# First channel group of the pooling mixer: pooled without scale and shift, both applied later, and TensorE, ScalarE and VectorE in written order there

## The chip, the core and the metric

The kernel runs on one core of a Trainium2 chip. The metric is the device time of one execution in microseconds (us), the median of several. Engines: TensorE (PE) multiplies matrices, VectorE (DVE), ScalarE (ACT) and GpSimd (POOL) work elementwise, SyncE (SP) issues the DMA transfers from HBM.

## What is computed

Two layers of a backbone over 256 latent tokens and 256 context tokens with 2048 channels, float32. Layer 0 mixes tokens by pooling in four channel groups of 512 (windows 2, 4, 8, 16), layer 1 by attention; a gated MLP with a depthwise convolution follows each. What matters here is the start of layer 0:

```python
ml = (silu_c @ w_mod[i] + b_mod[i]).reshape(B, 6, 1, D)      # shift, scale, gate; shift, scale, gate
mc = (silu_cc @ w_mod[i] + b_mod[i]).reshape(6, 1, 1, D)
a_lat = modulate(rms_norm(h, norm1_g[i]), ml[:, 0], ml[:, 1])   # x * (1 + scale) + shift
...
parts.append(window_sum / count[None, :, None] - ug)          # pool_mix, per channel group
y = jnp.einsum('btgc,gcd->btgd', p, w).reshape(B, T, D) + b
return y * scale
...
h = h + ml[:, 2] * y_lat
h = h + ml[:, 5] * conv_ffn(modulate(rms_norm(h, norm2_g[i]), ml[:, 3], ml[:, 4]), ...)
```

The pooling is linear along the tokens, and scale and shift are one number per channel: pool(s * x + t) = s * pool(x) + t * pool(1).

## The kernel before

Channels lie on the 128 partitions: a stream (latent `hl`, context `hc`) is 16 tiles of 128 x 256, and both streams are worked on together as 128 x 512. Float32 products are made of three matmuls with high and low parts (hi x hi, hi x lo, lo x hi); `split` (L143, L145) makes the parts of weights with a cast on ScalarE and a difference on VectorE.

The modulation is a product with w_mod, 24 chunks of 512 channels. `mod_pe` makes one chunk: eight loads ("pieces") of 512 KB, `wm{layer}_{chunk}_{g}_{0 or 1024}`; each piece gives two matmuls with 32 columns of output each (L193), and the piece `..._0` fills other columns of the array (j = 0, 1) than `..._1024` (j = 2, 3). The bank is then evicted by ScalarE (L198, `modev`), transposed by TensorE (L203, `modt`), reduced and biased on VectorE (L205, L181, and L183 for scales) to `modT`. Chunk 4w + g belongs to group g; w = 0 is the shift, 1 the scale, 2 the gate, 4 the second scale; 12 + g is the second shift. `mods()` lists the chunks, `need(n)` advances this list to its n-th step of four per chunk.

`mixer(g)` pools one group: `py` = h x scale x rs1 on VectorE (L453; rs1 is one over the norm), the shift added by ScalarE into a zero-padded row `pad` (L455), window sums `ws` on VectorE (L461), times one over the count on GpSimd (`pf`, L466), minus the middle (L467), high and low parts `ph` (L469, L470). Then 48 matmuls with the pooling weights `wp` (`pm`, L484 to L486), eviction with gate and bias by ScalarE (`pz`, L491), the addition to h by GpSimd (L493), squares for the second norm (`n2q`, L276), and `Ad`, h times the second scale in two parts (L502, L503). `partial(g)` multiplies `Ad` with the first columns of the MLP's weights (`cg`, `cu`, L545 to L547), and in between calls `need` and the next step of the next group's mixer; `pw` (L528) and `pt` (L561) are its products with the second shift.

Loads go through SP's queue in order, into "rooms" (`stage`): 6 of a pool of their own and those of the tiles A0 to A15 that `lend` names. A load waits until the last user of its room is done. The order of all engines is set by a planner that works on the list of operations with estimated times; nothing in this part is written out by hand.

Of the kernel before, what the change touches and what calls it, by code (L numbers as in the profile page):

```python
# [10 lines left out]
F32 = mybir.dt.float32  # L11
F32R = mybir.dt.float32r
# [45 lines left out]
def kernel(ctx: ExitStack, tc: tile.TileContext, xT, cxT, wmod, wg, wu, wd, wp,  # L58
# [264 lines left out]
    with ExitStack() as ph0:  # L323
# [62 lines left out]
        with ExitStack() as phs:  # L386
# [4 lines left out]
            n1 = Norm(both, f0, "n1")  # L391
            for k in range(KT):
                n1.add(h_of, k)
            pr = n1.rstd()
            rs1 = st.tile([P, 512], F32, bufs=1, name="rs1")
            nc.scalar.copy(rs1, pr)
# [42 lines left out]

            def mixer(g):  # L440
# [4 lines left out]
                gsc = st.tile([P, 8], F32, bufs=1, name=f"gsc{g}")  # L445
                gbi = st.tile([P, 8], F32, bufs=1, name=f"gbi{g}")
                pa = []
                for i in range(4):
# [7 lines left out]
                    src, w = pad, 1  # L456
                    while w < win:
                        n = WP - 2 * w + 1
                        if w == 1:
                            dst = st.tile([P, 2, WP], F32, tag="ws", name=f"ws{k}")  # L460
                        nc.vector.tensor_tensor(dst[:, :, :n], src[:, :, :n], src[:, :, w : w + n], op=ALU.add)  # L461
                        src, w = dst, 2 * w
                    o = PAD - win // 2
                    pf = f0.tile([P, 2, T], F32, tag="t2", name=f"pf{k}")
                    for s in both:
                        nc.gpsimd.tensor_tensor(pf[:, s, :], src[:, s, o : o + T], inv_t, op=ALU.mult)  # L466
                    nc.vector.tensor_tensor(pf, pf, pad[:, :, PAD : PAD + T], op=ALU.subtract)  # L467
                    ph = ap0.tile([P, 2, 2, T], F32R, tag=f"A{k}", name=f"ph{k}")
                    nc.scalar.copy(ph[:, 0], pf)  # L469
                    nc.vector.tensor_tensor(ph[:, 1], pf, ph[:, 0].bitcast(F32), op=ALU.subtract)  # L470
                    pa.append(ph)
                    if i == 3:
                        parts = ld(wp[g], f"wp{g}")
                    yield
                nc.vector.tensor_tensor(gsc, modT[0, 8 + g].rearrange("p i s -> p (i s)"), V("ps")[:, 8 * g : 8 * g + 8],
                                        op=ALU.mult)
                nc.vector.tensor_tensor(gbi, gsc, V("pb")[:, 8 * g : 8 * g + 8], op=ALU.mult)
                for m in range(4):
                    ps = bank("d", f"pm{g}_{m}")
                    for i in range(4):  # L480
                        hi, lo = parts[i // 2]
                        c = 512 * (i % 2) + P * m
                        rh, rl = flat(pa[i][:, 0]), flat(pa[i][:, 1])
                        nc.tensor.matmul(ps, hi[:, c : c + P], rh, start=(i == 0), stop=False)  # L484
                        nc.tensor.matmul(ps, hi[:, c : c + P], rl, start=False, stop=False)
                        nc.tensor.matmul(ps, lo[:, c : c + P], rh, start=False, stop=(i == 3))  # L486
                    k = 4 * g + m
                    y = f0.tile([P, 2, T], F32, tag="t2", name=f"pz{k}")
                    for s in both:
                        j = 2 * m + s  # L490
                        nc.scalar.activation(y[:, s], ps[:, T * s : T * s + T], AF.Identity,  # L491
                                             scale=gsc[:, j : j + 1], bias=gbi[:, j : j + 1])
                        nc.gpsimd.tensor_tensor(h_of(s)[:, k, :], h_of(s)[:, k, :], y[:, s], op=ALU.add)  # L493
                    n2.add(h_of, k)
                    if m % 2:
                        yield

# [714 lines left out]
```

## Time and profile before

| | |
|---|---|
| median of 3 runs | 3119.4 us (3118.2 to 3119.62) |
| the profiled execution | 3121.16 us, its span 3119.4 us |
| mean granted TensorE clock | 0.992 |
| TensorE waiting for pieces of w_mod | 25.3 us in 14 waits, the longest 19.0 us (the start) |
| HBM read | 554.93 MB, 179 GB/s over the span |

The profile is of one execution. Times are counted from the start of its span. A row of the timeline or of the chain has a start, a duration, an engine, a line and tiles (output<-inputs, with buffer numbers left out); x8 is eight instructions of the profiler, and a float32 matmul shows as two, so a whole piece of w_mod is x4. A name after "<-" at the end is what the engine waited for.

### The profile page before, as it was taken

What the parts mean: (1) busy time and instruction counts of PE and PEld (TensorE: products, weight loads), DVE (VectorE), ACT (ScalarE), POOL (GpSimd) and SP (SyncE); (2) the same over time, 40 slices, a digit from 0 to 9 for tenths busy, and PEclk for the clock granted to TensorE, in tenths of its full rate; (3) what the DMA queues carried; (4) which work ended last, traced back from release to release, by engine and by line L of the source; (5) the groups of instructions that cost most, each with busy time, mean ns of one, the idle gap of its engine ahead of it and who ended that gap; (6) DMA issues with size and microseconds to landing.
All of it is one profiled execution on the core that took longest, in us unless ns stands there. A gap on an engine that the chain in (4) does not pass through costs nothing.

```text
span 3119.4 us, 40851 instructions
## 1 busy us (share of the span) xinstructions
PE 3038.2 (97%) x15082; PEld 2410.6 (77%) x15082; DVE 1937.9 (62%) x2726; ACT 1371.9 (44%) x2219; POOL 874.7 (28%) x845
## 2 busy tenths in 40 slices
PE   6999899999999999999999999999999999999998
PEld 2565558888888888888887888878878888888887
DVE  4445674285765858557485665474767666666666
ACT  3333455323233332333334444343545556566665
POOL 2011213203031130312203000000002576667776
PEclk9999999999999999999999999999999999999999
DMA  9888573374746648476572333333345556555553
GB/s 377 331 273 311 177 237 95 95 231 143 239 150 201 205 148 255 136 215 185 168 249 86 104 113 101 105 110 109 107 149 183 179 173 201 188 183 182 176 191 114
DMA packets 177928, 559.71 MB, mean 179 GB/s; under 512 B 17600, under 2 KB 22208, under 8 KB 177728
## 3 DMA queue, kind: packets, MB, share of 16 engines
q1 hardware_dynamic: 177728, 557.10, 55.1%
q8 instruction: 119, 1.95, 0.2%
q14 instruction: 81, 0.66, 0.1%
HBM read 554.93 MB, written 2.10 MB: 179 GB/s over the span
## 4 chain that ended last, share of the span: by engine, by line
PE 93%; POOL 2%; DVE 2%; DMA 2%; issue 1%; ACT 1%; SPq 0%; DVEq 0%; POOLq 0%; ACTq 0%
PE g L764 5%; PE d L657 5%; PE d L659 5%; PE d L658 5%; PE u L764 5%; PE d L809 4%; PE u L631 4%; PE u L632 4%; PE u L633 4%; PE g L631 4%; PE g L633 4%; PE g L632 4%; PE mod L193 3%; PE g L765 3%; PE u L765 2%; PE d L810 2%
## 5 line engine op out<-in xcount | busy, mean ns | idle before, releaser
L670 POOL TENSOR_TENSOR hl<-hl,dy 128x256 f32<-128x256 f32 x160 | 149.5, 934 | 957.1 <-ACT dy L669 955.9
L241 DVE SCALAR_TENSOR_TENSOR macc<-wm,sc,macc 128x512 f32<-128x512 f32 (+1 forms) x360 | 325.3, 935 | 69.2 <-DMA wm<-wmod 68.0
L821 POOL TENSOR_TENSOR hl<-hl,dy 128x256 f32<-128x256 f32 x320 | 321.3, 1035 | 45.7 <-ACT dy L819 44.1
L669 ACT ACTIVATE dy<-d,modT 128x256 f32<-128x256 f32 x320 | 133.7, 471 | 196.0 <-PE d L659 194.7
L193 PE MATMUL mod<-wm,sc 128*32 128x512 f32 x768 | 135.0, 611 | 25.3 <-DMA wm<-wmod 25.3
L670 POOL TENSOR_TENSOR hc<-hc,dy 128x256 f32<-128x256 f32 x160 | 127.0, 794 | 0.0
L145 DVE TENSOR_TENSOR wd_2l<-wd,wd_2h 128x1024 fp32r<-128x1024 f32 (+1 forms) x44 | 54.8, 1251 | 102.7 <-ACT wd_2h L143 101.8
L819 ACT ACTIVATE dy<-d,modT 128x512 f32<-128x512 f32 x160 | 103.6, 686 | 30.7 <-PE d L810 30.6
L908 POOL TENSOR_TENSOR rk<-rk,rp 128x256 f32<-128x256 f32 x16 | 13.8, 861 | 365.7 <-DVE rk L907 302.0
L466 POOL TENSOR_TENSOR pf<-ws,inv 128x256 f32<-128x256 f32 x32 | 27.8, 887 | 223.8 <-DVE ws L461 156.0
L145 DVE TENSOR_TENSOR wd_3l<-wd,wd_3h 128x1024 fp32r<-128x1024 f32 (+1 forms) x33 | 40.0, 1216 | 80.6 <-ACT wd_3h L143 80.5
L193 PEld LDWEIGHTS mod<-wm,sc 128*32 128x32 f32 x768 | 23.7, 109 | 80.8 <-issue 57.7
L788 DVE TENSOR_TENSOR actb<-sgb,actb 128x256 fp32r<-128x256 f32 x43 | 71.7, 1669 | 21.2 <-ACT actb L787 20.0
L145 DVE TENSOR_TENSOR wd_0l<-wd,wd_0h 128x1024 fp32r<-128x1024 f32 (+1 forms) x44 | 53.7, 1228 | 45.1 <-ACT wd_0h L143 44.3
L143 ACT CAST wd_1h<-wd 128x1024 fp32r<-128x1024 f32 (+1 forms) x44 | 45.2, 1029 | 78.6 <-PE u L632 55.5
L994 ACT ACTIVATE sb<-sb,nm 128x512 f32<-128x512 f32 x64 | 46.2, 722 | 63.1 <-DVE nm L990 61.4
L143 ACT CAST wd_0h<-wd 128x1024 fp32r<-128x1024 f32 (+1 forms) x44 | 45.2, 1030 | 59.9 <-PE u L764 27.9
L145 DVE TENSOR_TENSOR wd_1l<-wd,wd_1h 128x1024 fp32r<-128x1024 f32 (+1 forms) x33 | 40.0, 1214 | 45.8 <-ACT wd_1h L143 45.8
L657 PE MATMUL d<-act,wd_2h 128*128 128x512 f32 x172 | 68.0, 395 | 0.0
L658 PE MATMUL d<-act,wd_2h 128*128 128x512 f32 x172 | 67.9, 395 | 0.0
L657 PE MATMUL d<-act,wd_3h 128*128 128x512 f32 x172 | 67.9, 395 | 0.0
L659 PE MATMUL d<-act,wd_2l 128*128 128x512 f32 x172 | 67.9, 395 | 0.0
(1754 smaller groups left out, 10074.1 us busy)
## 6 DMA issues: line engine op xcount, KB each, us to landing
wm<-wmod SPq DMA_DIRECT2D x384, 512.0 KB, 6.1
wd<-wd SPq DMA_DIRECT2D x168, 512.0 KB, 4.6
wg<-wg SPq DMA_DIRECT2D x156, 512.0 KB, 4.3
wu<-wu SPq DMA_DIRECT2D x156, 512.0 KB, 4.8
wv<-wv SPq DMA_DIRECT2D x32, 512.0 KB, 3.7
wk<-wq SPq DMA_DIRECT2D x32, 512.0 KB, 3.8
wq<-wq SPq DMA_DIRECT2D x32, 512.0 KB, 3.7
wo<-wo SPq DMA_DIRECT2D x32, 512.0 KB, 4.0
```

What stands on the lines that cost most here:

```text
L145: eng.tensor_tensor(lo[:, :n], t[:, :n], hi[:, :n].bitcast(F32), op=ALU.subtract)
L193: nc.tensor.matmul(ps[32 * j : 32 * j + 32, :], sc[:, 4 * g + j, :], ts[j // 2][0][:, 512 * (j % 2) : 512 * (j % 2) + 512], start=(g == 0) ...
L241: nc.vector.scalar_tensor_tensor(acc[s], v, sc2[:, k, s : s + 1], acc[s], op0=ALU.mult, op1=ALU.add)
L631: nc.tensor.matmul(ps, hi[:, c : c + P], xh, start=(k == 0), stop=False)
L632: nc.tensor.matmul(ps, hi[:, c : c + P], xl, start=False, stop=False)
L633: nc.tensor.matmul(ps, lo[:, c : c + P], xh, start=False, stop=(k == KT - 1))
L657: nc.tensor.matmul(ps, hi[:, o : o + P], xh, start=(i == 0), stop=False)
L658: nc.tensor.matmul(ps, hi[:, o : o + P], xl, start=False, stop=False)
L659: nc.tensor.matmul(ps, lo[:, o : o + P], xh, start=False, stop=(i == n - 1))
L670: nc.gpsimd.tensor_tensor(h_of(s)[:, k, :], h_of(s)[:, k, :], y[:, s], op=ALU.add)
L764: nc.tensor.matmul(ps, hi[:, c : c + P], flat(B[k]), start=(k == 0), stop=False)
L821: nc.gpsimd.tensor_tensor(hl[:, k, :], hl[:, k, :], y[:, q], op=ALU.add)
```

## The change

1. In the first group the chunk order is scale, shift, gate, second scale, second shift (4, 0, 8, 16, 12) instead of 0, 4, 8, 16, 12.
2. `first_mixer` takes the place of `mixer(0)`. It pools h x rs1, without scale and shift. `z` is the pooled row of ones minus one (three small operations on VectorE at the start). The scale is applied by ScalarE in place to the pooled tile, shift x z is added by VectorE. The pooled tiles lie in the rooms A4 and A5, `z` in A6, so that `lend` gives 15 rooms instead of 18 up to the first `partial`.
3. The first norm and all of `first_mixer` stand in a block in which PE, Activation and DVE keep the written order. The pm matmuls go over four banks at once, one pooled tile after the other, with chunk 8's pieces in between; the loads of `wp` stand ahead of chunk 8's, and all of `Ad` ahead of the squares.
4. `mixer` for the other groups does what it did, in helper functions; `gsc` and `gbi` have two buffers.

```diff
@@ -419,7 +414,7 @@
                 for g in range(4):
-                    for w in (0, 1, 2, 4):
+                    for w in (0, 1, 2, 4) if g else (1, 0, 2, 4):
                         yield from mod_pe(0, 4 * w + g, sc, f0)
                     yield from mod_pe(0, 12 + g, sc, f0)
                     shifts(g)
@@ -437,13 +432,146 @@
+            def windows(pad, win, name):
...
+            def means(pf, pad, inv_t, win, name):
+                src, o = windows(pad, win, name)
+                for s in both:
+                    nc.gpsimd.tensor_tensor(pf[:, s, :], src[:, s, o : o + T], inv_t, op=ALU.mult)
+
+            def less(pf, pad):
+                nc.vector.tensor_tensor(pf, pf, pad[:, :, PAD : PAD + T], op=ALU.subtract)
+
+            def high(pf, k):
+                ph = ap0.tile([P, 2, 2, T], F32R, tag=f"A{k}", name=f"ph{k}")
+                nc.scalar.copy(ph[:, 0], pf)
+                return ph
+
+            def low(pf, ph):
+                nc.vector.tensor_tensor(ph[:, 1], pf, ph[:, 0].bitcast(F32), op=ALU.subtract)
...
+            def add_pooled(g, m, ps, gsc, gbi):
+                k = 4 * g + m
+                y = f0.tile([P, 2, T], F32, tag="t2", name=f"pz{k}")
+                for s in both:
+                    j = 2 * m + s
+                    nc.scalar.activation(y[:, s], ps[:, T * s : T * s + T], AF.Identity,
+                                         scale=gsc[:, j : j + 1], bias=gbi[:, j : j + 1])
+                    nc.gpsimd.tensor_tensor(h_of(s)[:, k, :], h_of(s)[:, k, :], y[:, s], op=ALU.add)
+
+            def scaled(k):
...
+            def first_mixer():
+
+                win = POOL_WINDOWS[0]
+                inv_t = st.tile([P, T], F32, bufs=1, tag="inv", name="inv0")
+                nc.sync.dma_start(inv_t, inv[:, 0, :])
+
+                z = ap0.tile([P, 1024], F32, tag="A6", name="z")[:, 0:T]
+                one = pads[1][:, 0:1]
+                nc.gpsimd.memset(one[:, :, PAD : PAD + T], 1.0)
+                src, o = windows(one, win, "wz")
+                nc.vector.tensor_tensor(z, src[:, 0, o : o + T], inv_t, op=ALU.mult)
+                nc.vector.tensor_scalar(z, z, -1.0, None, op0=ALU.add)
+                rooms2 = [ap0.tile([P, 2, 2, T], F32, tag=f"A{4 + j}", name=f"pf{j}") for j in range(2)]
+                pfs = [rooms2[k // 2][:, k % 2] for k in range(4)]
+                n1 = Norm(both, f0, "n1")
+                for k in range(KT):
+                    n1.add(h_of, k)
+                need(1)
+                pr = n1.rstd()
+                nc.scalar.copy(rs1, pr)
+
+                def begin(k):
+                    pad = pads[k % 2]
+                    for s in both:
+                        nc.vector.tensor_tensor(pad[:, s, PAD : PAD + T], h_of(s)[:, k, :], rs1[:, T * s : T * s + T],
+                                                op=ALU.mult)
+                    means(pfs[k], pad, inv_t, win, f"ws{k}")
+
+                def scale(k):
+                    for s in both:
+                        v = pfs[k][:, s, :]
+                        nc.scalar.activation(v, v, AF.Copy, scale=M(0, 1, k, s))
+
+                begin(0)
+                begin(1)
+                need(5)
+                less(pfs[0], pads[0])
+                begin(2)
+                scale(0)
...
+                need(8)
+                ts = load(lambda a, b: wp[0][:, a:b], 2048, "wp0")
+                need(9)
...
+                banks = [bank("gu", f"pm0_{m}") for m in range(4)]
+                parts, pa = [], []
+                for k in range(4):
+                    if k % 2 == 0:
+                        parts += split(ts[k // 2 : k // 2 + 1], f"wp0_{k}")
+                    for s in both:
+                        v = pfs[k][:, s, :]
+                        nc.vector.scalar_tensor_tensor(v, z, M(0, 0, k, s), v, op0=ALU.mult, op1=ALU.add)
+                    pa.append(high(pfs[k], k))
+                    low(pfs[k], pa[k])
+                for k in range(4):
+                    for m in range(4):
+                        pool_mm(banks[m], parts, pa, k, m)
+                    if k < 3:
+                        need(10 + k)
+                need(13)
+                gsc, gbi = gates(0)
+                for m in range(4):
+                    add_pooled(0, m, banks[m], gsc, gbi)
+                need(17)
+                for k in range(4):
+                    scaled(k)
+                for k in range(4):
+                    n2.add(h_of, k)
@@ -567,11 +664,10 @@
-            lend(range(4, KT))
-            mix = mixer(0)
-            for n in STEPS:
-                need(n + 2)
-                next(mix)
+            lend(range(7, KT))
+            with tc.manual_schedule(engines={mybir.EngineType.PE, mybir.EngineType.Activation, mybir.EngineType.DVE}):
+                first_mixer()
+            need(19)
```

Three places of the order show what moves. A row is a line, an operation, output<-inputs and a shape; `mod_16` is chunk 16's bank, `wm_16_1_1024` its fourth piece, and a number at a name's end counts tiles.

TensorE in the first group's pooling matmuls, before (the four pooled tiles are ph_333, ph_347, ph_361 and ph_375):

```order
L484 MATMUL pm_0_435<-ph_375,wp0h_386 128x512
L193 MATMUL mod_16_408<-wm_16_1_1024_419,sc 32x512 x2
L485 MATMUL pm_0_435<-ph_375,wp0h_386 128x512
L486 MATMUL pm_0_435<-ph_375,wp0l_387 128x512
L485 MATMUL pm_1_457<-ph_361,wp0h_386 128x512
L486 MATMUL pm_1_457<-ph_361,wp0l_387 128x512
L193 MATMUL mod_16_408<-wm_16_2_0_425,sc 32x512 x2
L484 MATMUL pm_1_457<-ph_375,wp0h_386 128x512
```

and in the change (the first tile is ph_364, the second ph_369):

```order
L466 MATMUL pm_3_357<-ph_364,wp_0h_358 128x512
L467 MATMUL pm_3_357<-ph_364,wp_0h_358 128x512
L468 MATMUL pm_3_357<-ph_364,wp_0l_359 128x512
L193 MATMUL mod_8_340<-wm_8_1_0_398,sc 32x512 x2
L193 MATMUL mod_8_340<-wm_8_1_1024_400,sc 32x512 x2
L466 MATMUL pm_0_354<-ph_369,wp_0h_358 128x512
L467 MATMUL pm_0_354<-ph_369,wp_0h_358 128x512
```

Before, chunk 16's pieces stood among the pooling matmuls, which went bank by bank; now all four banks take one pooled tile, and two pieces of chunk 8 stand between one tile and the next. Chunk 16 follows behind.

TensorE at the start of the gate matmuls, before:

```order
L203 MATMUL modt_16_533<-ident,modev_16_531 128x128 x4
L193 MATMUL mod_12_542<-wm_12_0_0_543,sc 32x512 x2
L193 MATMUL mod_12_542<-wm_12_0_1024_545,sc 32x512 x2
L193 MATMUL mod_12_542<-wm_12_1_0_551,sc 32x512 x2
L193 MATMUL mod_12_542<-wm_12_1_1024_553,sc 32x512 x2
L193 MATMUL mod_12_542<-wm_12_2_0_559,sc 32x512 x2
L193 MATMUL mod_12_542<-wm_12_2_1024_561,sc 32x512 x2
L545 MATMUL cg_0_599<-Ad_567,wcg_0h_591 128x512
L545 MATMUL cg_1_614<-Ad_567,wcg_0h_591 128x512
```

and in the change:

```order
L193 MATMUL mod_12_536<-wm_12_2_0_590,sc 32x512 x2
L193 MATMUL mod_12_536<-wm_12_2_1024_592,sc 32x512 x2
L193 MATMUL mod_12_536<-wm_12_3_0_632,sc 32x512 x2
L642 MATMUL cg_0_610<-Ad_545,wcg_0h_602 128x512
L642 MATMUL cg_1_625<-Ad_545,wcg_0h_602 128x512
L193 MATMUL mod_12_536<-wm_12_3_1024_634,sc 32x512 x2
L643 MATMUL cg_0_610<-Ad_545,wcg_0h_602 128x512
```

The last two pieces of chunk 12 stood among the gate matmuls; now the seventh stands ahead of them and the eighth behind the first two.

TensorE in the third group, chunk 18's last pieces, before:

```order
L547 MATMUL cu_4_1823<-Ad_1320,wcu_4l_1805 128x512
L193 MATMUL mod_18_1761<-wm_18_2_0_1880,sc 32x512 x2
L193 MATMUL mod_18_1761<-wm_18_2_1024_1882,sc 32x512 x2
L193 MATMUL mod_18_1761<-wm_18_3_0_1941,sc 32x512 x2
L193 MATMUL mod_18_1761<-wm_18_3_1024_1943,sc 32x512 x2
L545 MATMUL cu_5_1873<-Ad_1293,wcu_4h_1804 128x512
```

and in the change:

```order
L644 MATMUL cu_5_1882<-Ad_1331,wcu_4l_1814 128x512
L193 MATMUL mod_18_1770<-wm_18_3_0_1952,sc 32x512
L466 MATMUL pm_0_1901<-ph_1860,wp2h_1871 128x512
L466 MATMUL pm_1_1923<-ph_1860,wp2h_1871 128x512
L193 MATMUL mod_18_1770<-wm_18_3_0_1952,sc 32x512
L467 MATMUL pm_0_1901<-ph_1860,wp2h_1871 128x512
L468 MATMUL pm_0_1901<-ph_1860,wp2l_1872 128x512
L467 MATMUL pm_1_1923<-ph_1860,wp2h_1871 128x512
L468 MATMUL pm_1_1923<-ph_1860,wp2l_1872 128x512
L193 MATMUL mod_18_1770<-wm_18_3_1024_1954,sc 32x512 x2
```

What was one run of four pieces is cut: pieces five and six stand by themselves further up, the seventh is in two single rows and the eighth apart, between matmuls of the pooling.

More of the change, by code (lines that the diff above doesn't have):

```diff
@@ L455, in mixer @@
                         nc.scalar.activation(pad[:, s, PAD : PAD + T], y[:, s], AF.Identity, bias=M(0, 0, k, s))
[L456 to L463, printed above, removed]
-                    pf = f0.tile([P, 2, T], F32, tag="t2", name=f"pf{k}")
[L465 to L471, printed above, removed]
+                    pf = f0.tile([P, 2, T], F32, tag="t2", name=f"pf{k}")
+                    means(pf, pad, inv_t, win, f"ws{k}")
+                    less(pf, pad)
+                    pa.append(high(pf, k))
+                    low(pf, pa[i])
                     if i == 3:
@@ L474, in mixer @@
                     yield
[L475 to L477 removed]
+                gsc, gbi = gates(g)
                 for m in range(4):
@@ L480, in mixer @@
                     for i in range(4):
[L481 to L494, printed above, removed]
+                        pool_mm(ps, parts, pa, i, m)
+                    add_pooled(g, m, ps, gsc, gbi)
+                    n2.add(h_of, 4 * g + m)
                     if m % 2:
```

50 lines of the change are left out of this document (36 added, 14 removed).

## Prediction

> **What bounds the kernel now.** I read the page first (span, busy time, the chain that ended last), then the granted clock and the DMA share by stretch, then the chain and the timeline of the first 90 us, where the change lies.
>
> ```profile
> span 3119.4 us, 40851 instructions
> PE 3038.2 (97%) x15082; PEld 2410.6 (77%) x15082; DVE 1937.9 (62%) x2726; ACT 1371.9 (44%) x2219; POOL 874.7 (28%) x845
> PE 93%; POOL 2%; DVE 2%; DMA 2%; issue 1%; ACT 1%; SPq 0%; DVEq 0%; POOLq 0%; ACTq 0%
> ```
>
> TensorE is busy 97% of the span and 93% of the chain: the kernel is a queue of matmuls. A change of the order of work elsewhere pays only where TensorE waits, and it costs wherever it lengthens TensorE's own queue. The stretches show where it waits:
>
> ```profile
> 20.00:40.00 20.00, 17.01 (x87) 5.01 (x85) 3.07 (x11) 1.76 (x3) 1.03 (x1) 1.00 1.03 408
> 40.00:60.00 20.00, 13.86 (x51) 4.36 (x50) 16.44 (x29) 8.70 (x15) 6.71 (x8) 0.83 1.03 408
> 60.00:80.00 20.00, 18.55 (x98) 9.12 (x96) 5.53 (x10) 10.35 (x23) 5.69 (x8) 1.00 0.96 363
> 80.00:100.00 20.00, 20.00 (x112) 11.29 (x111) 6.76 (x13) 7.63 (x13) 0.00 (x0) 1.00 0.98 335
> ```
>
> The columns are the busy time of PE, PEld, DVE, ACT and POOL, then the clock, the DMA share and GB/s. From 20 to 60 us the DMA engines are full (1.03, 408 GB/s) and TensorE is not; VectorE is nearly full only from 40 to 60 (16.44 of 20), which is the first group's pooling. From 80 us TensorE has no gap left. So the change can win only what lies before that point: it must bring TensorE to its gapless state earlier. The chain says what holds it there:
>
> ```profile
> 53.37 0.61 DVE pf L467
> 55.16 0.66 PE modt L203 x4
> 57.18 0.73 PE pm L484
> 62.22 0.99 PE mod L193 x8
> 63.21 0.43 PE pm L484
> 63.64 0.98 PE mod L193 x4
> 74.40 0.57 ACT pz L491
> 76.13 0.58 ACT modev L198
> 76.75 0.66 PE modt L203 x4
> 77.41 2.71 PE mod L193 x24
> 80.12 0.66 PE cg L545 x2
> ```
>
> Columns: start, duration, what. VectorE's pooling lets the pooling matmuls (pm) start at 57.2 only; they end at 74.2, chunk 16 (the second scale) is transposed behind them at 76.75, and the first group's gate matmuls (cg) begin at 80.1.
>
> **The change in the first 80 us.** The chunk order puts the scale first, and the pooling no longer needs either chunk, only rs1. In the old kernel VectorE has the room for it:
>
> ```profile
> 40.49 0.19 DVE L205 TENSOR_REDUCE modT<-modt 128x8 f32<-128x32 f32 x1 [9.78 <-PE modt L203]
> 41.20 0.48 DVE L453 SCALAR_TENSOR_TENSOR py<-hl,modT,rs 128x256 f32<-128x256 f32 x1
> L470 DVE TENSOR_TENSOR ph<-pf,ph 128x512 fp32r<-128x512 f32 x4 | 3.2, 798 | 0.0
> L145 DVE TENSOR_TENSOR wp0l<-wp,wp0h 128x1024 fp32r<-128x1024 f32 x2 | 2.4, 1210 | 0.0
> L469 ACT CAST ph<-pf 128x512 fp32r<-128x512 f32 x4 | 2.5, 618 | 4.4 <-DVE pf L467 4.4
> L491 ACT ACTIVATE pz<-pm,gbi,gsc 128x256 f32<-128x256 f32 x8 | 4.1, 561 | 8.7 <-PE pm L486 8.7
> L143 ACT CAST wcg_0h<-wcg 128x1024 fp32r<-128x1024 f32 x2 | 2.1, 1034 | 0.0
> L493 POOL TENSOR_TENSOR hl<-hl,pz 128x256 f32<-128x256 f32 x4 | 2.9, 730 | 13.3 <-ACT pz L491 13.3
> ```
>
> VectorE idles 9.78 us before 40.5; most of the new products, window sums and differences go there. Added are eight shift products (0.48 each alone, as the py row) and three small operations for z ahead of everything, removed are eight ACT pad operations against eight ACT scalings: about 4 us more on VectorE, hidden by that idle time; without it the pm stage would be 4 us later, which the cover named below still takes. After the shift chunk is ready (41 us, one small load later than the 40.5 above), what is left per tile is two products, a cast and a difference: 2 x 0.48 + 0.62 + 0.80 = 2.4 us, plus two low parts of the weights at 1.21. I put the first tile of ph at 47 and the last at 55, against pm's start at 57.2.
>
> A pm tile is now 12 matmuls, 2.8 us at the 0.23 us that the last fence of this part shows, and between tiles stands a pair of chunk 8's pieces (1.2 us): 47 + 4 x 2.8 + 3 x 1.2 = 61.8 us for the end of pm. The eight pz then take about 4 us on ScalarE, ending at 66.6; chunk 16's eviction is queued behind them, so its transpose stands at about 67.2 instead of 76.75. GpSimd's eight additions (0.73 each) end at 69. All this has some 5 us of cover, because cg needs something else first: its weights and the last pieces of chunk 12, and those come with the DMA stream.
>
> ```profile
> 49.95 3.12 PE L193 MATMUL mod<-wm,sc 128*32 128x512 f32 x8 [2.80 <-DMA wm<-wmod]
> 64.08 15.15 SPq L127 DMA_DIRECT2D wm<-wmod  x8
> 88.08 0.60 PE L203 MATMUL modt<-ident,modev 128*128 128x128 f32 x4
> ```
>
> At 49.95 TensorE took a piece as it landed: chunk 8's seventh, the 36th entry of SP's queue. Chunk 12's last two are the 55th and 56th in both orders, and the same loads stand ahead of them. A load of 512 KB takes 1.285 us at 408 GB/s; 18 of these and one quarter-size load give 49.9 + 23.4 = 73.3, and 74.6 for the other (the gate's weights, one and two places ahead, by 70.8 and 72.1). The queue itself is no limit: the old one spreads eight issues over 15.15 us from 64.08, waiting for rooms that chunk 16 frees at 74 to 75, and the new one frees them at 63 to 66, although it has 15 rooms instead of 18 there. So the sum for the first stretch: piece 55 is used at 73.4 to 74.4, two cg matmuls follow, piece 56 at 74.7 to 75.7, then the other 22 cg matmuls at 0.43 + 21 x 0.23 = 5.3. **Chunk 12 is transposed at 81.0 instead of 88.08: a gain of 7.0 us.** The order on VectorE (both low parts of the gate weights now ahead of Ad's) fits beneath: 72.1 + 1.03 for the cast + 1.21 = 74.3, before piece 56.
>
> One doubt is the clock. It can drop in the gap before piece 55, between the block of 24 (67.9 + 2.7 = 70.6) and 73.4: 2.8 us.
>
> ```profile
> 50.00:52.00 2.00, 2.00 (x6) 0.33 (x8) 2.00 (x4) 1.35 (x3) 1.76 (x2) 0.50 1.03 410
> 58.00:60.00 2.00, 2.00 (x6) 1.55 (x6) 1.44 (x6) 0.62 (x1) 0.00 (x0) 0.58 1.03 406
> ```
>
> In the old trace a wait of 2.80 us (the row at 49.95) was followed by a clock of 0.50 for about 3 us. The same here would cost half of 3 us, 1.5; none if the clock holds. I take 0.7, since the work ahead of this gap is denser: a gain of 6.3. (The Trainium skill, "TensorE: Matmul & The Clock Gate", section "HAM oscillation — how this bites in real kernels", says that idle gaps over about 3.4 us throttle the array again; by it the gap would cost nothing and the gain would be 7.0. The 2.80 us row above speaks against so sharp a bound.)
>
> **What is given back later.** The planner sets the order anew up to the last group, and it cuts the pieces of w_mod differently. What a cut costs shows in the third group, where chunk 18 is made:
>
> ```profile
> 236.53 0.84 PE mod L193 x6
> 238.73 0.24 PE cu L547
> 238.96 0.97 PE mod L193 x2
> 239.94 0.43 PE cu L545
> 240.37 0.24 PE cu L546
> 241.54 1.85 PE mod L193 x16
> ```
>
> One row of a piece (x2) takes 0.97 us; a whole piece (x4, 63.64) 0.98; two pieces together (x8, 62.22) 0.99; four (x16) 1.85; six (x24, 77.41) 2.71. The left and right half of a row run side by side on the array, so a run costs 0.12 + 0.86 for each pair, full or not, and the matmul behind it takes 0.43 instead of 0.23. An additional run that splits a pair costs about 1.18 us. By the orders there are 51 runs from chunk 1 to chunk 15 before, and 57 now. Priced one by one: chunk 5 +1.2 (one run becomes two), 9 -0.3, 17 -1.2, 10 +0.6, 18 +2.7 (four become seven), 3 +0.3, 15 +1.2, the others 0; **sum +4.5 us**, on an engine without gaps. Bounds: 0 if all of the additional runs fall into waits, 7 if each of the six costs its full price. The nearest row for waits is this one:
>
> ```profile
> 220.00:240.00 20.00, 18.56 (x105) 11.13 (x104) 19.39 (x33) 8.63 (x14) 4.13 (x4) 1.00 0.87 292
> ```
>
> TensorE waits only 1.4 us there, so I stay with 4.5. From chunk 20 on the order is the same, and nothing there is tied to a fixed moment: a shift passes through to the end.
>
> **Sum.** 3119.4 (the span; the profiled execution took 3121.16 with what lies around it, and the median of the three runs is 3119.4 too) - 6.3 + 4.5 = **3117.6 us**.
>
> **Rivals.** (a) The gain stays: the additional runs fill waits (1.4 us at 220 to 240, and chunk 6's last piece is 18 rows earlier in the new order, which gives the third group's pooling 4 us more), and the clock holds: 3119.4 - 7.0 = 3112.4. For it: the early gain rests on landings, the loss only on counting. Against: the rows at 237 to 243 have no gap in which a run is free. (b) Slower: VectorE becomes the bound of the third group's start. At 220 to 240 it is busy 19.39 of 20, and in the new order two pm tiles there alternate matmul by matmul on the last pooled tile, with single rows of chunk 18 between. If that tile comes late, TensorE stops at each. The kernel is slower by over 0.2% once such waits exceed 6.3 - 4.5 + 6.2 = 8 us; with 8.5, 3126. For it: that stage has the least room on VectorE. Against: its pooling can begin earlier, as said in (a). (c) The change moves the pooling but not the start of cg: the stream of loads sets it in both kernels. Then 3119.4 plus some of the cuts less a wait or two, about 3120. Against: the chain names pm, pz and the transpose at 76.75, while the last pieces were there by 75.
>
> **How the numbers follow.** Forecast 0.42, own range 3113.5 to 3121.5 (gain 5 to 7, loss 1 to 7). Rival (a) 0.33, (b) 0.20, (c) 0.05. A measurement of this kernel can tell about 0.2%, 6.2 us, from no change: 3113.2 and 3125.6 are the borders. (a) lies below, (b) above, the rest between, with a little of the forecast's own range beyond the lower border: faster 0.35, same 0.44, slower 0.21. The range 3109.5 to 3127 holds (a) with some waits filled besides, and (b) down to its border and somewhat above.
>
> **What would show it.** Right: cg begins near 74.5 and chunk 12's transpose stands near 81; TensorE is gapless from about 75; chunk 18's pieces make seven runs of about 1 us each. Wrong: cg after 78 (the early sum), a clock of 0.5 at 74 to 78 (the doubt), a TensorE busy time of the stretch 80 to 360 that needs no more microseconds for the same rows (the cuts), or waits for DVE on pm rows near 240, which would make it rival (b).

## The result, and the profile after

The changed kernel takes 3125.95 us (median of 8 executions, 3123.24 to 3129.32), the kernel before beside it 3119.28 (8 executions, 3116.59 to 3121.05): a ratio of 1.0023, 95% interval [1.0013, 1.0032]. It is 6.7 us slower, where the forecast was 1.8 us faster. The profiled execution is one of the eight (3125.9 us). Its span is 4.7 us longer than the one before, not 6.7, since the profiled execution of the kernel before (3121.16 us) lies 1.9 us above its median:

```profile
span 3124.1 us, 40845 instructions
PE 3031.1 (97%) x15082; PEld 2412.4 (77%) x15082; DVE 1926.8 (62%) x2737; ACT 1370.7 (44%) x2219; POOL 873.7 (28%) x846
```

TensorE is busy 7.1 us less than before (3031.1 against 3038.2) in the longer span: it waits 12 us more. The stretches of the changed kernel, with the columns of the prediction's table, show where:

```profile
20.00:40.00 20.00, 10.19 (x38) 4.77 (x38) 11.09 (x22) 7.34 (x20) 1.02 (x1) 1.00 0.92 366
40.00:60.00 20.00, 11.64 (x70) 4.43 (x63) 13.78 (x26) 7.76 (x14) 6.17 (x8) 0.89 0.95 355
60.00:80.00 20.00, 18.58 (x103) 10.08 (x101) 4.89 (x11) 5.92 (x13) 3.41 (x5) 0.94 0.90 323
```

From 20 to 40 us TensorE works 10.19 us instead of 17.01, and the loads, at 1.03 and 408 GB/s before, have fallen to 0.92 and 366. This is earlier than anything that the prediction counted. What stands at the beginning of it is seen on VectorE. In the timeline of the kernel before, the 14 additions of the first norm's squares begin at 10.66:

```profile
10.66 11.05 DVE L282 TENSOR_TENSOR n1q<-n1q,n1q 128x512 f32<-128x512 f32 x14 [5.81 <-ACT n1q L276]
```

In the timeline of the changed kernel the same row stands behind `z`:

```profile
4.75 0.43 DVE L442 TENSOR_TENSOR wz<-pad 128x271 f32<-128x271 f32 x1
18.14 0.43 DVE L506 TENSOR_TENSOR z<-wz,inv 128x256 f32<-128x256 f32 x1 [12.95 <-DMA inv<-inv]
18.81 11.03 DVE L282 TENSOR_TENSOR n1q<-n1q,n1q 128x512 f32<-128x512 f32 x14
```

The second of the "three small operations" reads inv0. That load is the eleventh entry of SP's queue, behind the eight loads of the inputs, and lands at 18.1. VectorE has nothing to do in those 12.95 us, because its next instructions in the written order are the additions, and they stand behind `z`. The squares that they need were there: the kernel before takes the first at 10.66. The norm is 8.15 us late (18.81 against 10.66), and TensorE, in written order too, stands in front of it. Its timeline in the changed kernel:

```profile
29.90 3.58 PE L289 MATMUL n1s<-ones,n1q 128*128 128x1 f32 x16 [7.33 <-DVE n1q L282]
35.95 2.07 PE L299 MATMUL n1b<-n1d,ones 128*128 128x512 f32 x2 [2.48 <-DVE n1d L297]
37.96 4.81 PE L193 MATMUL mod<-wm,sc 128*32 128x512 f32 x24
...
56.98 0.80 PE L466 MATMUL pm<-ph,wp_0h 128*128 128x512 f32 x1 [6.25 <-ACT ph L456]
...
74.41 0.60 PE L203 MATMUL modt<-ident,modev 128*128 128x128 f32 x4
...
80.23 0.66 PE L203 MATMUL modt<-ident,modev 128*128 128x128 f32 x4 [1.64 <-ACT modev L198]
...
84.37 0.73 PE L642 MATMUL cg<-Ad,wcg_0h 128*128 128x512 f32 x2
...
91.15 0.60 PE L203 MATMUL modt<-ident,modev 128*128 128x128 f32 x4
```

It waits 7.33 us for the additions, then 2.48 for the norm, with the other six pieces of chunk 4 behind them; the kernel before uses four pieces at 23.9. The pooling matmuls come at 57.0 instead of 47, chunk 8 is transposed at 74.41, chunk 16 at 80.23 (before 76.75, forecast 67.2). The gate matmuls begin at 84.37 (before 80.05, forecast about 74.5), and chunk 12 is transposed at 91.15 (before 88.08, forecast 81.0, or 81.8 with the 0.7 for the clock). The first 12 pm rows run at 0.43 us each, since the clock fell in the 6.25 us of waiting:

```profile
58.00:60.00 2.00, 2.00 (x5) 1.52 (x5) 1.13 (x3) 1.52 (x2) 0.00 (x0) 0.50 1.03 412
```

The late pieces free their rooms late, so the loads slip as well. The gate's weights are issued by SP like this, before and after:

```profile
60.26 1.65 SPq L127 DMA_DIRECT2D wcg<-wg  x2
```

```profile
72.08 4.33 SPq L127 DMA_DIRECT2D wcg<-wg  x2
```

TensorE does not wait for these loads: up to chunk 12 its one wait for a load is that for its first piece, at 19.46.

Behind chunk 12 stand the cuts of w_mod's pieces. Between chunk 12's and chunk 15's transposes both kernels execute the same matmuls. Before, that stretch reads

```profile
88.08:362.91 274.83, 272.73 (x1519) 165.90 (x1518) 141.25 (x246) 99.73 (x177) 42.98 (x49) 1.00 0.79 278
```

and after

```profile
91.15:369.34 278.19, 277.17 (x1520) 165.86 (x1519) 139.55 (x246) 99.52 (x177) 40.60 (x49) 1.00 0.77 279
```

TensorE is busy 4.44 us longer (277.17 - 272.73), and 1.1 us of waiting is gone (2.10 against 1.02); the stretch grows by 3.35. So the account of this pair of traces is +3.1 up to chunk 12 and +3.35 up to chunk 15; at chunk 23's transposes it is +6.40 (458.45 against 452.05), and the rest of the span takes 1.7 us less, which is within what two traces of one kernel differ by (3.3 us there in z_cast and cast_again, below). The +3.1 is also of the size of that scatter; the 4.44 us of TensorE's time are not.

### The profile page after: what moved, and what is told of

It reads as the page before. It is cut to its first block, busy times and chain, and to the rows that moved or that the text cites. A ratio compares the mean times of both kernels' runs of the same rounds, so it can differ in the third digit from the quotient of the medians.

```text
span 3124.1 us, 40845 instructions
## 1 busy us (share of the span) xinstructions
PE 3031.1 (97%) x15082; PEld 2412.4 (77%) x15082; DVE 1926.8 (62%) x2737; ACT 1370.7 (44%) x2219; POOL 873.7 (28%) x846
## 4 chain that ended last, share of the span: by engine, by line
PE 93%; POOL 2%; issue 2%; DVE 2%; DMA 1%; ACT 1%; DVEq 0%; POOLq 0%; SPq 0%; ACTq 0%
PE g L860 5%; PE d L753 5%; PE d L755 5%; PE d L754 5%; PE u L860 4%; PE d L905 4%; PE u L727 4%; PE u L728 4%; PE u L729 4%; PE g L727 4%; PE g L729 4%; PE g L728 4%; PE mod L193 3%; PE g L861 3%; PE u L861 2%; PE d L906 2%
## 5 line engine op out<-in xcount | busy, mean ns | idle before, releaser
L193 PE MATMUL mod<-wm,sc 128*32 128x512 f32 x768 | 128.6, 617 | 21.3 <-DMA wm<-wmod 21.3
L884 DVE TENSOR_TENSOR actb<-sgb,actb 128x256 fp32r<-128x256 f32 x43 | 62.0, 1443 | 19.8 <-ACT actb L883 19.3
L753 PE MATMUL d<-act,wd_0h 128*128 128x512 f32 x172 | 67.9, 395 | 0.0
```

The source lines that it names most:

```text
L193: nc.tensor.matmul(ps[32 * j : 32 * j + 32, :], sc[:, 4 * g + j, :], ts[j // 2][0][:, 512 * (j % 2) : 512 * (j % 2) + 512], start=(g == 0) ...
L753: nc.tensor.matmul(ps, hi[:, o : o + P], xh, start=(i == 0), stop=False)
```

## The experiments

Two questions: is it `z`'s wait that costs the beginning, and what else keeps the forecast gain away. The table has the starts of the transposes of chunks 16, 12, 15 and 23 in each trace; up to each of these marks all kernels run the same matmuls (but for the fillers of the last two, and four gate matmuls that b_wait does behind chunk 12 instead of ahead of it, 0.9 us). The kernel before was run beside each batch, at 3119.0 (rows 3 to 6), 3119.33 (7 to 9) and 3118.87 (10 to 12).

| kernel | chunk 16 | chunk 12 | chunk 15 | chunk 23 | span | median | ratio to before |
|---|---|---|---|---|---|---|---|
| before | 76.75 | 88.08 | 362.91 | 452.05 | 3119.4 | 3119.28 | |
| the change | 80.23 | 91.15 | 369.34 | 458.45 | 3124.1 | 3125.95 | 1.0023 [1.0013, 1.0032] |
| z_late | 73.22 | 91.92 | 370.06 | 458.10 | 3123.9 | 3125.38 | 1.0019 [1.001, 1.0028] |
| no_manual | 71.40 | 89.48 | 369.66 | 458.85 | 3123.9 | 3128.01 | 1.0028 [1.0019, 1.0037] |
| b_wait | 80.50 | 90.95 | 367.69 | 455.90 | 3123.2 | 3122.47 | 1.0011 [1.0003, 1.002] |
| z_rev | 72.96 | 91.24 | 375.60 | 460.60 | 3128.4 | 3134.66 | 1.0049 [1.0037, 1.0061] |
| z_cast | 70.39 | 84.92 | 362.37 | 450.12 | 3117.7 | 3121.60 | 1.0005 [0.9996, 1.0014] |
| n1_cast | 71.88 | 86.41 | 363.75 | 454.37 | 3120.4 | 3121.33 | 1.0003 [0.9995, 1.0012] |
| inv_cast | 73.22 | 87.76 | 365.07 | 454.52 | 3120.8 | 3122.55 | 1.0007 [0.9998, 1.0016] |
| cast_again | 71.99 | 86.51 | 363.99 | 453.49 | 3117.8 | 3121.29 | 1.0004 [0.9995, 1.0012] |
| z_warm | 71.44 | 86.00 | 363.59 | 452.62 | 3120.1 | 3117.71 | 0.9994 [0.9986, 1.0003] |
| warm_norm | 70.88 | 85.39 | 362.79 | 451.52 | 3117.0 | 3117.59 | 0.9992 [0.9983, 1.0001] |

**z_late: z behind the norm.** The six lines of `z` (room, row of ones, three operations) move below the norm and its copy; everything else is the change.

```diff
-                z = ap0.tile([P, 1024], F32, tag="A6", name="z")[:, 0:T]
...
                 nc.scalar.copy(rs1, pr)
+                z = ap0.tile([P, 1024], F32, tag="A6", name="z")[:, 0:T]
+                one = pads[1][:, 0:1]
...
+                nc.vector.tensor_scalar(z, z, -1.0, None, op0=ALU.add)
```

> The three operations for z are written behind the first norm instead of ahead of it; nothing else is changed. Theory A (VectorE waits for inv0, and the norm's 14 additions are queued behind that wait): the additions start near 10.7 us instead of 18.8, the norm's TensorE part stands near 22 instead of 29.9, pm starts near 47 to 49, chunk 12 is transposed at 81 to 84 instead of 91.15, and the kernel takes 3115 to 3119 us. Theory B (the stage is slow by its written order and a half clock at pm, the wait is hidden behind the loads): chunk 12's transpose stays at 88 or later and the kernel at 3123 or more.

The wait is gone and chunk 16 comes at 73.22, 7.0 us earlier than in the change and 3.5 earlier than before. But chunk 12 comes at 91.92, and the time does not move. These are theory B's numbers and not its mechanism, since the first wait was worth 7.0 us at chunk 16: a second wait has taken the gain. ScalarE's timeline in z_late:

```profile
75.22 0.51 ACT L491 ACTIVATE Ad<-hl,modT 128x256 fp32r<-128x256 f32 x1 [2.06 <-DVE modT L183]
...
80.57 0.40 ACT L276 ACTIVATE n2q<-hc 128x256 f32<-128x256 f32 x1
80.88 1.98 ACT L143 CAST wcg_0h<-wcg 128x1024 fp32r<-128x1024 f32 x2
```

and the first gate matmul on its TensorE:

```profile
81.96 0.80 PE L642 MATMUL cg<-Ad,wcg_0h 128*128 128x512 f32 x1 [5.37 <-ACT wcg_0h L143]
```

The planner had set the casts of the gate's weights ahead of `Ad` in the change; with `z` moved it sets them behind the whole written block, that is behind 8 scalings and 8 squares for a norm that nobody waits for yet. TensorE stands 5.37 us and then runs at a clock of 0.50 up to 86:

```profile
82.00:84.00 2.00, 2.00 (x6) 1.16 (x7) 2.00 (x3) 0.86 (x1) 0.00 (x0) 0.50 1.01 401
```

**no_manual: the change without the written order.** The block's `with` line is taken away; the planner orders all three engines.

```diff
-            with tc.manual_schedule(engines={mybir.EngineType.PE, mybir.EngineType.Activation, mybir.EngineType.DVE}):
-                first_mixer()
+            first_mixer()
```

> The change without the block of written order: the planner orders TensorE, ScalarE and VectorE there too, and puts z's product behind 11 of the 14 additions. Theory A: at most 1 us of the wait is left, chunk 12's transpose at 82 to 85, and with cuts priced 1.5 us above those of the change 3117 to 3121 us. Theory B: the written order costs, not the wait; then this one is faster than z_late by 2 us or more.

The additions begin at 10.47, as before: VectorE now does 11 of them ahead of `z`, whose load has landed by then.

```profile
19.05 0.42 DVE L506 TENSOR_TENSOR z<-wz,inv 128x256 f32<-128x256 f32 x1
```

So the written order, not `z` as such, made the first wait. The time is no better, and both theories had it lower: 3128.01 us, 2.6 more than z_late. TensorE's trace has two other waits, for ScalarE's evictions and for the same casts (total, times, longest):

```profile
PE modt L203 <- ACT modev L198: 8.8, 4, 6.0
PE cg L642 <- ACT wcg_0h L143: 4.7, 1, 4.7
```

The longest eviction wait lies ahead of chunk 16, which still comes 8.8 us earlier than in the change. Behind chunk 16 stand the wait for the casts and more cuts: from chunk 12 to chunk 15 TensorE is busy 279.49 us, 2.3 more than in the change. The rest of the difference is not accounted for.

**b_wait: the suspected wait alone, put into the kernel before.** inv0 is loaded behind the inputs, and one VectorE operation on it stands ahead of the additions.

```diff
...
+            inv_0 = st.tile([P, T], F32, bufs=1, tag="inv", name="inv0")
+            nc.sync.dma_start(inv_0, inv[:, 0, :])
+            first = nc.vector.tensor_scalar(rs1[:, 0:T], inv_0, -1.0, None, op0=ALU.add)
             n1 = Norm(both, f0, "n1")
-            for k in range(KT):
-                n1.add(h_of, k)
+            with tc.issue_after(first.ins):
+                for k in range(KT):
+                    n1.add(h_of, k)
...
```

> The kernel before, with the load of inv0 right behind the inputs and one VectorE operation on it ahead of the first norm's additions; the operation's result is not used. Theory A with the cover that the old pooling has (it needs the scale chunk, at 41 us, so the norm may come 10 us later): the additions start near 18 us, chunk 12's transpose moves by less than 2 us, and the kernel stays within 3 us of before (the order prices the cuts 1.8 us higher). Rival (such a wait is paid wherever it stands): 8 us slower, 3127.

VectorE's timeline repeats the picture of the change:

```profile
17.42 0.29 DVE L394 TENSOR_SCALAR rs<-inv 128x256 f32<-128x256 f32 x1 [12.37 <-DMA inv<-inv]
17.63 11.04 DVE L282 TENSOR_TENSOR n1q<-n1q,n1q 128x512 f32<-128x512 f32 x14
```

Chunk 12 is 2.87 us late (3.8 with the four gate matmuls) and the kernel 3.5 us slower, both more than expected. The old kernel has cover for the norm, since the planner put pieces of chunk 4 between, yet not for all of it. The planner also made the cuts anew (+1.9 from chunk 12 to 15, 0.9 of it those four), so the 3.5 are not the wait's alone.

**z_rev: the halves of a piece's pair in the other order** (on z_late). A run of pieces then begins with the half that lands last, and pairs are no longer split; the cuts were priced 7.4 us lower.

```diff
-            for j in range(4):
+            for j in (2, 3, 0, 1):
```

> As z_late, and each pair of pieces of w_mod is multiplied right half first (j = 2, 3, 0, 1), so that the first matmul of a pair waits for both loads. By the order this leaves 73 runs of pieces from chunk 1 on instead of 80; priced as in the prediction 105.1 us instead of 112.5. Theory C (a cut costs TensorE time as priced): 7 us faster than z_late, within 2. Rival (cuts fall into waits, or the order alone does not count): within 2 us of z_late.

This expectation failed. Between chunk 12's and chunk 23's transposes TensorE is indeed busy 7.3 us less (349.33 against 356.59 in z_late), but it now waits for loads. The waits of z_late in that stretch, with the columns total, times, longest, and then those of z_rev:

```profile
PE pwu L625 <- DMA wcu<-wu: 3.9, 2, 2.5
PE mod L193 <- DMA wm<-wmod: 0.9, 2, 0.7
```

```profile
PE mod L193 <- DMA wm<-wmod: 8.4, 4, 3.3
PE pwu L625 <- DMA wcu<-wu: 5.5, 2, 3.8
```

The price of a cut is real as TensorE's time, but a whole pair waits for the half that lands last. The stretch is 3.2 us longer than in z_late (369.36 against 366.18). The median is 9.3 us above z_late's; the traced execution is the fastest of the six, and where the rest is lost is not shown.

**z_cast: z_late, with the gate's first weights cast ahead.** Load and casts of wcg0_0 move from `partial` into the written block, ahead of the scalings.

```diff
                 need(17)
+                ts0 = load(lambda a, b: wg[0, a // 512 : b // 512, :, 0:512].rearrange("f p c -> p f c"), 2048, "wcg0_0")
+                EARLY.append((ts0, split(ts0, "wcg0_0")))
                 for k in range(4):
                     scaled(k)
...
```

> z moved behind the norm as in z_late, and besides the first gate weights wcg0_0 loaded and cast inside the written block, ahead of the scaling Ad and of the second norm's squares, instead of behind them. Theory (z_late lost its gain to ScalarE's written order: the gate matmuls waited 5.4 us for a cast that stood behind 16 operations): modt16 stays near z_late's 73.2, the wait before the gate matmuls goes and modt12 comes at 82 to 86 instead of 91.9 (88.1 before); the cuts are priced at 109.2 us against 108.5 before and 112.5 in z_late, so the kernel ends 1 to 5 us under before: 3114 to 3118. Rival (whatever comes early is given back to the load stream or to the half clock): modt12 not before 88, kernel 3119 to 3122.

The early part came as the theory has it, the time is above its range. ScalarE casts at 70.2, and Ad follows:

```profile
70.17 2.05 ACT L143 CAST wcg_0h<-wcg 128x1024 fp32r<-128x1024 f32 x2
72.41 0.51 ACT L491 ACTIVATE Ad<-hl,modT 128x256 fp32r<-128x256 f32 x1 [0.18 <-DVE modT L183]
```

TensorE starts pm at 48.0, transposes chunk 16 at 70.39, begins the gate matmuls at 73.36, about where the forecast has them, and transposes chunk 12 at 84.92:

```profile
47.99 0.79 PE L466 MATMUL pm<-ph,wp_0h 128*128 128x512 f32 x1 [2.29 <-ACT ph L456]
...
70.39 0.66 PE L203 MATMUL modt<-ident,modev 128*128 128x128 f32 x4 [1.65 <-ACT modev L198]
...
73.36 0.74 PE L649 MATMUL cg<-Ad,wcg_0h 128*128 128x512 f32 x2 [0.48 <-ACT Ad L491]
...
84.92 0.66 PE L203 MATMUL modt<-ident,modev 128*128 128x128 f32 x4 [0.79 <-ACT modev L198]
```

The kernel is 4.4 us faster than the change and cannot be told from the one before. Between chunk 12 and chunk 15 TensorE is busy 2.4 us longer than before:

```profile
84.92:362.37 277.45, 275.13 (x1519) 164.43 (x1519) 141.93 (x246) 98.51 (x175) 44.20 (x49) 1.00 0.77 274
```

**inv_cast: z where the change has it, inv0 loaded ahead of the inputs.** The casts are as in z_cast.

```diff
+            inv_0 = st.tile([P, T], F32, bufs=1, tag="inv", name="inv0")
+            nc.sync.dma_start(inv_0, inv[:, 0, :])
             for g in range(4):
                 nc.sync.dma_start(hl[:, 4 * g : 4 * g + 4, :], xT[:, 4 * g : 4 * g + 4, :])
...
-                inv_t = st.tile([P, T], F32, bufs=1, tag="inv", name="inv0")
-                nc.sync.dma_start(inv_t, inv[:, 0, :])
+                inv_t = inv_0
```

> The change with z left where it was, ahead of the norm, but with inv0 loaded ahead of the 16 input tiles, and with the gate weights' casts ahead as in z_cast. Theory (z cost nothing by itself, only by its wait for a transfer that lands behind the inputs): the norm additions start near 10.7 as before, and the whole is within 2 us of z_cast. Rival (it is the three operations or the window sum themselves, or the order of VectorE as such, that delay the norm): the additions start late again, near 18, and modt16 comes near 80 as in the change.

As the theory has it: `z` is done by 6.2, and the additions start at 11.02.

```profile
5.41 0.42 DVE L509 TENSOR_TENSOR z<-wz,inv 128x256 f32<-128x256 f32 x1
...
11.02 2.29 DVE L282 TENSOR_TENSOR n1q<-n1q,n1q 128x512 f32<-128x512 f32 x3 [4.86 <-ACT n1q L276]
```

Chunk 16 comes at 73.22, 7.0 us before the change's, and the median is 0.95 us from z_cast's. The operations are the same three in the same place; only the landing of their operand differs.

**n1_cast: z_cast with the norm outside the written block,** its `Norm`, additions and copy moved ahead of the `with` line, unchanged.

> As z_cast, and the first norm stands outside the written block, as it did before the change, so that its squares take inputs in the order of arrival and mod pieces stand between the two norm matmul groups. Theory (the written order of the norm costs the stage 2 to 4 us: TensorE stands between n1s and n1b and then runs 24 piece matmuls at the half clock): first scale at the time of before (modt at 29 to 31), modt16 at 68 to 71 instead of 73.2, modt12 at 79 to 83, kernel 3111 to 3115. Rival (modt16 and modt12 hang on the loads, not on the norm): no earlier than z_cast within 1 us.

The theory failed. The additions start at 10.30, but now 16 rows of pieces stand between the two norm products, and the second of these comes no earlier than in z_cast (27.89 there):

```profile
25.17 3.64 PE L193 MATMUL mod<-wm,sc 128*32 128x512 f32 x16
28.74 1.99 PE L299 MATMUL n1b<-n1d,ones 128*128 128x512 f32 x2
```

Chunk 16 at 71.88 lies within the scatter of z_cast's two traces.

**cast_again: z_cast word for word.**

> z_cast once more, word for word, beside the two with fillers, for the scatter of its early stage: z_late and z_cast have the same order on TensorE up to chunk 16, but their modt16 differ, 73.2 and 70.4. Theory (the scatter comes from the landing of the first weight pieces, 18.8 or 19.8, and the clock that follows): modt16 at 70.4 or at 73.2, according to whether the first piece starts near 18.8 or 19.8. Rival (the cast and load order ahead matters): 70.4 again whatever the start. The time: 3119 to 3124 by either.

Chunk 16 at 71.99 against 70.39, with the first piece at 19.09 against 18.80; chunk 23 at 453.49 against 450.12, the spans 3117.8 and 3117.7. Neither outcome that I named was met exactly, but the order cannot be the cause, as it is the same. Where they first part clearly is the run of 24 piece rows behind n1b, 3.42 us in z_cast and here

```profile
30.19 4.49 PE L193 MATMUL mod<-wm,sc 128*32 128x512 f32 x24
```

Marks of single traces therefore scatter, here by 1.6 us at chunk 16 and 3.4 at chunk 23, and only larger differences are shown by one pair of traces. TensorE's busy time between two marks is far steadier: from chunk 12 to chunk 15 it is 275.13 us in z_cast and 275.10 here.

**z_warm: three matmuls that nobody reads, in TensorE's idle time ahead of pm** (on z_cast; they add work).

```diff
...
+                def keep_warm(n):
+                    for _ in range(n):
+                        nc.tensor.matmul(banks[3], ones, hl[:, 0:2, :].rearrange("p k t -> p (k t)"), start=True, stop=True)
+
+                keep_warm(1)
                 need(9)
+                keep_warm(2)
...
```

> As z_cast, with three matmuls of 128x512 whose result nobody reads put into TensorE's idle time ahead of the first pooled group: one ahead of chunk 0's transposes, two ahead of pm. The order behind them is z_cast's, and the cuts stay at 109.2 us. Theory (the pm group starts at half clock, with rows at 0.43 us instead of 0.23, because TensorE idles some 6 us of the 10 ahead of it, 8 to 12 rows of 0.2 each): all pm rows at 0.23, modt8 and modt12 1 to 2.4 us earlier than z_cast, less what the second filler delays pm. Rival (the half clock there comes from something else, the loads or the time since the start): pm rows at 0.43 again and modt12 the same or up to 2 us later.

The theory failed in its main point: the clock was still full when pm began, and fell all the same 2 us later.

```profile
48.88 0.50 PE L466 MATMUL pm<-ph,wp_0h 128*128 128x512 f32 x1 [2.70 <-ACT ph L456]
...
50.91 0.63 PE L466 MATMUL pm<-ph,wp_0h 128*128 128x512 f32 x1
```

pm started at the same moment as in cast_again (48.90), and chunk 8's transposes came 0.55 us earlier (65.63 against 66.18). That is all that the trace gives, and it does not explain the median, 3.6 us below cast_again's. The median's difference is clear of the noise all the same: the two kernels were run in one batch, and 9 of the 11 executions of z_warm lie under 3119 us, against 1 of the 11 of cast_again. The traced execution of z_warm is the slowest of its eleven (3121.84), so that where the gain arises is not shown.

**warm_norm: z_warm and one more filler between the two norm products.**

```diff
             pb = bank("d", f"{self.name}b")
+            if self.name == "n1":
+                nc.tensor.matmul(pb[:, : self.n], ones, self.last[:, : self.n], start=True, stop=True)
```

> As z_warm, with one more matmul nobody reads between the two groups of the first norm, where TensorE stands 2.5 us. Theory (that idle time is what puts the 24 piece matmuls behind n1b at half clock in z_late and inv_cast, 4.9 us instead of 3.4 in z_cast): they take 3.4 us or less in any case, and modt16 comes at 68 to 70.5. Rival (the clock of the pieces hangs on the idle start of the kernel, up to 18 us): 4.9 us is seen again, or the filler delays n1b by up to 1 us and nothing else moves.

The 24 rows take 3.62 us, against 4.49 in cast_again and the expected 3.4 or less:

```profile
25.59 2.05 PE L300 MATMUL n1b<-n1q,ones 128*128 128x512 f32 x2
...
30.22 3.62 PE L193 MATMUL mod<-wm,sc 128*32 128x512 f32 x24
```

Chunk 16 at 70.88 is 1.1 us ahead of cast_again's and misses the expected range by 0.4. In one trace this is within the scatter, as z_cast without a filler has 3.42 and 70.39. Of the 11 executions 9 lie under 3119 us, as in z_warm. At 3117.59 us the median is 8.4 us below the change and the lowest of the twelve, but against the kernel before it is 0.9992 with an interval that reaches 1.0001: no gain that these runs can tell.

## Why the prediction was wrong, point by point

**The step that failed** is "three small operations for z ahead of everything ... hidden by that idle time". I counted what they execute (0.43, 0.43 and 0.29 us in the trace) and put their wait at nothing. I did not ask what the second one waits for, where its load stands in SP's queue, and what is queued behind it on an engine that now keeps the written order. What the runs showed in its place is a wait of 12.95 us on VectorE, of which 8.15 reached the norm and 7.33 TensorE. inv_cast and z_late, which take away the wait in two different ways and keep the operations, both bring chunk 16 to 73.22, 7.0 us earlier. With this wait the gain of 6.3 fell out of the sum: chunk 12 came 3.1 us later than before. (The Trainium skill, "TensorE: Matmul & The Clock Gate", section "Architectural detail: the array is 16× 32×32, not 1× 128×128", calls ACT and DVE strict FIFO; the 14 additions, which begin at 18.81, right behind `z`, agree.)

**"The queue itself is no limit"** lost its reason with it. The claim held the rooms to be free at 63 to 66; they hang on the same late matmuls, and the gate's weights were issued at 72.08, 11.8 us later than before. TensorE did not wait for them, so that the claim itself was not put to the test.

**The chain pm to chunk 16** was built rightly and sized somewhat low. With the wait away pm starts at 48.0 (forecast 47) in z_cast, and from the end of pm to chunk 16's transposes pass 5.8 us (64.57 to 70.39; forecast 5.4). The pm block took 16.6 us instead of 14.8, mainly its first rows at 0.43. Here is the clock doubt of the prediction: the gap ahead of piece 55 that it named did not matter, those ahead of pm did.

**The gain of 6.3 at chunk 12** is not there even so: z_cast has 3.2 and cast_again 1.6. The gate matmuls begin in time there, at 73.36. What fails behind that is the assumption that only landings matter, so that one piece of chunk 12 would be left for the gate matmuls. In z_cast TensorE waits 0.48 and 0.34 us for `Ad` and 0.79 for chunk 12's eviction, 1.6 together, and takes chunk 12's pieces in five runs instead of two, 1.8 us more by the prediction's price. In z_late the casts behind ScalarE's written block take all of it.

**The cuts, +4.5,** were right in size: 4.44 us of TensorE's time, and chunk 18's seven runs are 2.7 of it, as priced (262.50 - 236.02 against 257.06 - 233.27). Of the waits, 1.1 us went, which the forecast had left in. In the other kernels the price by runs was mostly too low: by 0.7 to 0.8 us in z_late, no_manual and b_wait, and +2.4 us were measured for z_cast where +0.7 was priced; z_rev's -7.3 against z_late agrees with -7.4. That 4.5 and 4.44 agree so closely is therefore in part luck.

**The rivals.** (b) names almost the measured time, 3126, by luck, as its mechanism is not there: from 220 to 240 us TensorE of the changed kernel is busy 20.00 of 20. (a) and (c) did not come. That an operation ahead of the norm waits was none of the rivals.

**What stays open.** After both repairs the two traces show about -2 us at chunk 12 and +2.6 from there to chunk 15, which is nothing, and the ratios of z_cast and cast_again, 1.0005 and 1.0004, are nothing too. Why the fillers are worth 3.6 us was not settled, and neither was why the price by runs misses in z_cast.

## What to carry to other kernels

When engines are put in written order, each instruction that waits holds all that stands behind it: list, for every instruction moved to the front, the operand that lands last and its place in the load queue, and put whatever is needed last behind the work that is ready first. An operation costs its wait, not its duration. Write into the ordered block everything that the next stage on the same engines needs, since the planner may set the rest behind it; here a cast behind 16 operations cost as much as the first wait.

## What the runs showed of the hardware

- The granted clock falls after gaps of 2.7 us and less, and the fall can come when work has begun again. The stretches of z_warm behind its gap of 2.70 us:

```profile
48.00:50.00 2.00, 0.90 (x3) 0.54 (x4) 1.32 (x4) 0.62 (x1) 0.00 (x0) 1.00 1.01 401
50.00:52.00 2.00, 2.00 (x8) 1.59 (x7) 1.05 (x3) 1.57 (x2) 0.00 (x0) 0.70 1.05 418
```

  The fall comes 2 us after the matmuls have begun again. Two smaller gaps do it too, and here the clock falls within the second: in z_cast TensorE idles 1.15 us up to 40.09 and 1.84 us up to 42.59, with 0.7 us of transposes between, and the clock is at 0.50 in the work behind it (an estimate from the 0.87 puts the fall at 41.5):

```profile
40.00:42.00 2.00, 0.66 (x4) 0.42 (x4) 1.93 (x5) 0.46 (x3) 0.98 (x1) 0.87 1.02 412
42.00:44.00 2.00, 1.42 (x6) 0.41 (x8) 0.75 (x2) 1.09 (x4) 0.63 (x2) 0.50 1.02 408
```

  The rule of the Trainium skill that the prediction names (gaps over about 3.4 us throttle) is too sharp a bound for these. What the Trainium skill's page "TensorE: Matmul & The Clock Gate" says under "What's actually happening", that a free-running window judges how busy the array was, fits both.
- TensorE's first work is slow while the clock shown is 1.00. In the changed kernel n1s took 3.58 us (2.01 before), n1b 2.07 (1.13) and the 24 piece rows 4.81 (2.71 by the prediction's row), and the granted clock in the row from 20 to 40 above reads 1.00. The wait ahead of n1s is not the reason: in z_cast n1s stands right behind the first pieces, as in the kernel before, and takes as long:

```profile
21.83 3.58 PE L289 MATMUL n1s<-ones,n1q 128*128 128x1 f32 x16
```

```profile
22.00 2.01 PE L289 MATMUL n1s<-ones,n1q 128*128 128x1 f32 x16
```

  The first row is z_cast's, the second that of the kernel before; in every other trace n1s takes 3.09 us or more, so the trace of the kernel before is the exception, and why is open. The Trainium skill, "TensorE: Matmul & The Clock Gate", in "Seeing it yourself", warns that the traced clock events can be unreliable; these rows fit that, but that the clock makes them slow is not shown.
